# Seven block products for the down-projection of two FFN parts, with x streamed through DRAM

## The chip, the cores and the metric

One core of a Trainium2 chip runs one program. The metric is the device time of one execution in microseconds, and the verdict compares the kernel after with the kernel before on the same chip. Three runs of the kernel before are shown, and one profiled execution.

## What is computed

One step of a decoder trunk over 520 tokens (512 new ones of a sequence and 8 single ones) and a model width of 1024: half an FFN, a mixer of attention and state-space heads, half an FFN, a final norm. The change lies in the two FFNs, which are

```
h = rmsnorm(x, norm_g)
gate, up = split(h @ w_in)
x = x + 0.5 * ((silu(gate) * up) @ w_out)
```

with `w_in` of 1024 x 5632 and `w_out` of 2816 x 1024. All is float32 in and out.

## The kernel before

Everything is kept transposed: x is eight tiles of 128 features x 520 tokens, and the 2816 hidden features are 22 tiles `j`. A float32 product is made of three matmuls on TensorE: a value is split into a high part and a rest (`cut`, line 355, for weights: a cast on ACT, line 357, and a subtraction on DVE, line 358), and high x high, high x low and low x high are added in PSUM (`mm3`, lines 225 to 227; `product`, lines 579 to 581). Each matmul takes 128 x 128 weights and 260 tokens, half of the 520 (`HF`).

`ffn_comb` does one FFN. The hidden tiles come in four parts, `PARTS = ((0, 6), (6, 12), (12, 18), (18, 22))`. In each part the gate and up values of its tiles are computed, and then the part's share of the down-projection is added to x (the "down" stage, PSUM tiles `fo`, line 471 reads them). Tiles 0 to 4 use plain products. From tile 5 on (`SFROM`), gate and up are computed together as a 2 x 2 block product with seven multiplications in place of eight (Strassen's scheme in Winograd's form): `combos` prepares combinations of the normalised input once, `b_split` combinations of the weights for each `j`, and `comb_pair` (line 584) does the products 1, 5, 2, 6, 3, 7 in the PSUM banks `cx`, `cy`, `cz`; product 4 follows within the next pair or the down stage, in `comb_last` (line 608). Sums are kept in PSUM: bank x takes products 1, 6, 7 and 4 one after another, and between them ACT or DVE read it. After product 1, ACT copies x to bank z (line 590), after product 6 it copies x (line 596), and DVE reads x after product 7 (line 603) and after product 4 (line 612). The finished hidden tile is split again (`hidh`, line 615, and `hidl`, line 616).

The down stage of a part of six tiles takes 8 rows `m` of x, two halves, six tiles and three matmuls. Its weights come as eight "dn" units, 768 columns each, loaded as 512 and 256. Rows of x stay in SBUF: `reload` (line 1445) fetches all eight at the end of the first part, from the input or, in the second FFN, from the DRAM tile `spill`.

The order of TensorE's instructions is the order of the program text (`manual_schedule`); a scheduler orders the other engines and the DMA queues by program order and readiness, each queue in order. `stream` (line 303) lists the weight units with a cost; `b_more` (line 401) cuts further units while those cut and not yet taken are worth less than `AHEAD = 10` us; `b_load` (line 330) loads two units further. A pair's unit is five loads on SP's queue and two accumulating loads on POOL's (lines 350 to 352); DVE adds two more combinations (lines 384 and 386). The buffers are rings: 12 raw weight tiles (`r`), 14 + 12 cut ones (`q`, in the pools `pf` and `pg`), 58 general tiles of 528 columns (`t2`), and eight PSUM banks.

Of the kernel before, what the change touches and what calls it, by code (L numbers as in the profile page):

```python
# [14 lines left out]
T = 520  # L15
NP = 512
HF = 260
# [6 lines left out]
SRAW = 3  # L24
AHEAD = 10.0
# [60 lines left out]

def layout(inp):
# [5 lines left out]
    for n, s in (("ffn1", "1"), ("ffn2", "2")):  # L93
        out["wi" + s] = c(g[f"w_{n}_in"][0].reshape(8, 128, 2, 22, 128).transpose(3, 2, 1, 0, 4)).reshape(44, 128, 1024)
        out["wo" + s] = c(g[f"w_{n}_out"][0].reshape(22, 128, 8, 128).transpose(2, 1, 0, 3)).reshape(8, 128, 2816)
# [52 lines left out]
class Program:  # L148
# [147 lines left out]
    def stream(self, s):  # L296
        a = self.a
        wi, wo = a["wi" + s], a["wo" + s]
        u = []
        for lo, hi in PARTS:  # L300
            for j in range(lo, hi):
                if j < SFROM:
                    u += [("cl", wi[2 * j + i], 1024, 5.8) for i in range(2)]
                else:
                    u.append(("pair", wi[2 * j], wi[2 * j + 1], 10.1))
            if s == "1" and hi == PARTS[-1][1]:
                break
            u += [("dn", wo[m][:, lo * 128:hi * 128], (hi - lo) * 128, 0.72 * (hi - lo)) for m in range(8)]
        self.bu = u
        self.b_raw, self.b_w = {}, {}  # L310
        self.b_limit = 2 if s == "2" else len(u)
        self.b_first = 8 * (s == "2")
        self.b_q = self.b_loaded = self.b_cut = self.b_taken = 0

    def q2(self, name):
        n = self.b_q - self.b_first
        self.b_q += 1
        if self.qpool is not None:
            pool = self.qpool
        elif n < 0:  # L320
            pool = self.p0
        else:
            pool = self.pf if n < 12 or n % 7 % 2 == 0 else self.pg
        return pool.tile([128, 512], F32R, name=name, tag="q")

    def r2t(self, name):
        first = self.b_loaded <= 2 and self.b_first
        return (self.p0 if first else self.pf).tile([128, 512], F32, name=name, tag="r", bufs=4 if first else 12)

    def b_load(self):  # L330
# [15 lines left out]
        g, u = p  # L346
        h = slice(0, 512), slice(512, 1024)
        g0, s1, s3, g1, u1 = t = [self.r2t(f"br{n}_{i}") for i in range(5)]
# [12 lines left out]
    def b_split(self):  # L361
# [11 lines left out]
        else:  # L373
            g0, s1, s3, g1, u1 = raw
            s2, s4 = self.t2("s2"), self.t2("s4")
            w = {}
            ends = self.b_cut == len(self.bu), self.b_cut == len(self.bu) - 1
            if self.b_first == 0 and any(ends):
                self.qpool = self.pf
            w[1], w[5] = self.cut(g0), self.cut(s1)  # L380
            if self.b_first == 0 and ends[0]:
                self.qpool = self.pg
            w[2] = self.cut(g1)
            nc.vector.tensor_add(s2[:, :512], s1, g0)
            w[6] = self.cut(s2)
            nc.vector.tensor_add(s4[:, :512], s2[:, :512], g1)
            w[3], w[7] = self.cut(s4), self.cut(s3)
            if self.b_first == 0 and ends[1]:
                self.qpool = self.pg
            w[4] = self.cut(u1)  # L390
# [15 lines left out]
    def ffn_comb(self, gcol, source, after=None, early=None):  # L406
# [3 lines left out]
        with self.tc.manual_schedule(engines={mybir.EngineType.PE}):  # L410
            hid, held, r, norm = [], None, None, None
            for j in range(SFROM):
                pair = []
                if j == 0:
# [6 lines left out]
                    if self.b_first:  # L421
                        self.leave("p0")
                        self.enter("pg", 12, "right")
# [23 lines left out]
            prev = None  # L447
            for part, (lo, hi) in enumerate(PARTS):
                for j in range(max(lo, SFROM), hi):
                    prev = self.comb_pair(j, prev, hid)  # L450
                last = part == len(PARTS) - 1
                if part == 0:
                    self.reload(source)
                tail, prev = prev, None
                if last and after is None:
# [4 lines left out]
                for m in range(8):  # L460
                    w = self.w_take() if last else self.b_take()
                    ps = [self.bank1("fo") for _ in range(2)]
                    nk = hi - lo
# [5 lines left out]
                    for f in range(2):  # L469
                        x = self.x[m][:, f * HF:(f + 1) * HF]  # L470
# [8 lines left out]
                hid = []  # L479

    def to_mixer(self):

        self.leave("pf")
# [4 lines left out]
        for _ in range(2):  # L488
            self.w_split()

# [54 lines left out]
    def combos(self):  # L545
# [4 lines left out]
        for i in range(4):  # L550
            c = self.cx[i]
            c[1] = [t[:, a] for t in self.h[i]]
# [19 lines left out]
    def product(self, out, w, p, start):  # L572
# [3 lines left out]
        for i in range(4):  # L576
            xh, xl = self.cx[i][p]
# [3 lines left out]
            mm(out, lhsT=lo[:, ks], rhs=xh, start=False, stop=i == 3, skip_group_check=True)  # L581

    def comb_pair(self, j, prev, hid):
# [5 lines left out]
        self.product(x, w, 1, True)  # L589
        nc.scalar.copy(z, x)  # L590
        self.product(y, w, 5, True)
        nc.scalar.copy(pu[:, a], y)
        self.product(z, w, 2, False)
        nc.scalar.activation(c[:, a], z, AF.Silu)
        self.product(x, w, 6, False)
        nc.scalar.copy(pu[:, b], x)
        if prev is not None:
            self.comb_last(prev, hid)
        self.product(y, w, 3, False)
        nc.vector.tensor_add(c[:, b], y, pu[:, b])  # L600
        nc.scalar.activation(c[:, b], c[:, b], AF.Silu)
        self.product(x, w, 7, False)
# [3 lines left out]
        return x, w, c  # L606

    def comb_last(self, prev, hid):
        nc = self.nc
        x, w, c = prev  # L610
        self.product(x, w, 4, False)
        nc.vector.scalar_tensor_tensor(c[:, :HF], x, -1.0, c[:, :HF], ALU.mult, ALU.mult)
        hh = self.t2("hidh", F32R)
# [3 lines left out]
        hid.append((hh, hl))  # L617

# [901 lines left out]
    def run(self):  # L1520
        nc, tc, a = self.nc, self.tc, self.a
        with (
# [8 lines left out]
            self.enter("pf", 14)  # L1531
            self.enter("pg", 12, "right")
# [39 lines left out]
            def early():  # L1572
                self.leave("pg")
# [19 lines left out]
            self.enter("pf", 14)  # L1593
# [5 lines left out]
            self.leave("pg")  # L1599
            self.leave("pf")  # L1600
# [18 lines left out]
```

## Time and profile before

| what | us |
|---|---|
| median of the runs shown | 1125.81 |
| lowest and highest of the three | 1122.23, 1126.17 |
| the profiled execution | 1118.79 |
| its span in the profile | 1117.0 |
| TensorE busy | 1080.7 |
| VectorE busy | 719.4 |
| ScalarE busy | 501.6 |

The first FFN fills the span from about 8 us to 374 us, the mixer follows, and the second FFN runs from about 740 us to the end. In the rows, PE is TensorE's matmuls and PEld its weight loads, DVE is VectorE, ACT ScalarE, POOL GpSimd, and SPq a queue of DMA issues. A row of a timeline gives the start, the length and the instruction, in brackets the idle time before it and what ended it. Matmuls are pipelined and overlap in the records, and their ends are modelled.

### The profile page before, as it was taken

The page shows a single profiled execution, that of the slowest core. Times are in us where ns is not written, and L with a number is a line of the kernel's source. Part 1 is how long each engine was busy: PE and PEld are TensorE (multiplying, and loading weights), DVE is VectorE, ACT ScalarE, POOL GpSimd, SP SyncE. Part 2 cuts the span into 40 slices and gives each one's busy share as a digit, 9 for nine tenths or more (in the row PEclk, how much of TensorE's full clock was granted, in tenths as well). Part 3 has the DMA queues.
Part 4 walks back from the last instruction along what each step waited for, and adds up shares of the span by engine and source line. Part 5 has one row for each costly group of instructions (what it writes and reads, how often), then busy time and mean ns, then how long its engine had stood idle before and what let it go on. Part 6 is the DMA issues. An engine that isn't in the chain of part 4 may idle for free. (4 is left out here: it accounts for less than half of the span.)

```text
span 1117.0 us, 23260 instructions
## 1 busy us (share of the span) xinstructions
PE 1080.7 (97%) x9079; PEld 997.0 (89%) x9079; DVE 719.4 (64%) x1499; ACT 501.6 (45%) x1077; POOL 261.3 (23%) x261
## 2 busy tenths in 40 slices
PE   7999999999999999999989998999999999999995
PEld 6999999999999978676756776999999999999995
DVE  6985576467556678264677758449855774685563
ACT  6452454356245422356623554245533543562452
POOL 0001001010106668476234321030010011101013
PEclk8999999999999999899999997999999999999997
DMA  7538458456617889589899643264393584666302
GB/s 270 136 116 240 101 133 231 107 134 174 153 39 237 269 283 316 186 277 322 318 386 381 236 170 122 70 206 121 107 250 90 143 224 102 147 172 154 106 10 77
DMA packets 93917, 204.30 MB, mean 183 GB/s; under 512 B 13384, under 2 KB 21960, under 8 KB 89712
## 3 DMA queue, kind: packets, MB, share of 16 engines
q1 hardware_dynamic: 68736, 124.19, 34.1%
q0 software_dynamic: 22336, 77.08, 24.8%
q10 hardware_dynamic: 2736, 1.56, 0.5%
q8 instruction: 71, 1.16, 0.4%
q14 instruction: 38, 0.31, 0.1%
HBM read 191.78 MB, written 11.01 MB: 182 GB/s over the span
## 5 line engine op out<-in xcount | busy, mean ns | idle before, releaser
L357 ACT CAST qh<-br 128x512 fp32r<-128x512 f32 (+1 forms) x310 | 168.1, 585 | 121.0 <-PE fo L226 65.5
L358 DVE TENSOR_TENSOR ql<-br,qh 128x512 fp32r<-128x512 f32 (+1 forms) x310 | 189.2, 648 | 45.9 <-ACT qh L357 20.2
L226 PE MATMUL fo<-hidl,qh 128*128 128x260 f32 x640 | 181.3, 283 | 0.8 <-DVE hidl L616 0.8
L225 PE MATMUL fo<-hidh,qh 128*128 128x260 f32 x640 | 181.2, 283 | 0.0
L227 PE MATMUL fo<-hidh,ql 128*128 128x260 f32 x640 | 180.9, 283 | 0.0
L579 PE MATMUL cx<-ch,qh 128*128 128x260 f32 x544 | 153.7, 283 | 0.0
L581 PE MATMUL cx<-ch,ql 128*128 128x260 f32 x544 | 153.6, 282 | 0.0
L580 PE MATMUL cx<-cl,qh 128*128 128x260 f32 x544 | 153.6, 282 | 0.0
L226 PEld LDWEIGHTS fo<-hidl,qh 128*128 128x128 f32 x640 | 120.5, 188 | 1.5 <-DVE hidl L616 1.4
L225 PEld LDWEIGHTS fo<-hidh,qh 128*128 128x128 f32 x640 | 120.5, 188 | 0.0
L227 PEld LDWEIGHTS fo<-hidh,ql 128*128 128x128 f32 x640 | 120.5, 188 | 0.0
L225 PE MATMUL mps<-hh,whi 128*128 128x260 f32 x384 | 112.2, 292 | 1.6 <-DVE fdq L875 1.3
L351 POOL DMA_DIRECT2D br<-in_wi x34 | 29.7, 873 | 352.9 <-DMA br<-in_wi 232.2
L226 PE MATMUL mps<-hl,whi 128*128 128x260 f32 x384 | 108.6, 283 | 0.6 <-DVE hl L236 0.6
L227 PE MATMUL mps<-hh,wlo 128*128 128x260 f32 x384 | 108.4, 282 | 0.0
L579 PEld LDWEIGHTS cx<-ch,qh 128*128 128x128 f32 x544 | 102.4, 188 | 0.0
L581 PEld LDWEIGHTS cx<-ch,ql 128*128 128x128 f32 x544 | 102.4, 188 | 0.0
L580 PEld LDWEIGHTS cx<-cl,qh 128*128 128x128 f32 x544 | 102.3, 188 | 0.0
L789 POOL DMA_INDIRECT kv<-in_kc,ix x66 | 72.1, 1092 | 66.9 <-PE cy L581 25.7
L225 PEld LDWEIGHTS mps<-hh,whi 128*128 128x128 f32 x384 | 72.2, 188 | 13.4 <-issue 10.2
L579 PE MATMUL cy<-ch,qh 128*128 128x260 f32 x272 | 77.0, 283 | 0.0
L580 PE MATMUL cy<-cl,qh 128*128 128x260 f32 x272 | 77.0, 283 | 0.0
(430 smaller groups left out, 2721.9 us busy)
## 6 DMA issues: line engine op xcount, KB each, us to landing
br<-in_wi SPq DMA_DIRECT2D x206, 256.0 KB, 3.8
br<-in_wi POOLq DMA_DIRECT2D x68, 256.0 KB, 5.4
br<-in_wo SPq DMA_DIRECT2D x56, 256.0 KB, 2.9
wraw<-in_wm SPq DMA_DIRECT2D x24, 512.0 KB, 5.9
br<-in_wo SPq DMA_DIRECT2D x48, 128.0 KB, 2.7
kv<-in_kc SPq DMA_DIRECT2D x22, 256.0 KB, 4.3
spill<-xr SPq DMA_DIRECT2D x16, 260.0 KB, 2.0
xr<-spill SPq DMA_DIRECT2D x16, 260.0 KB, 5.1
```

The lines of the kernel that those rows point to most:

```text
L225: mm(out, lhsT=hi[:, ks], rhs=xh[:, cs], start=start, stop=False)
L226: mm(out, lhsT=hi[:, ks], rhs=xl[:, cs], start=False, stop=False)
L227: mm(out, lhsT=lo[:, ks], rhs=xh[:, cs], start=False, stop=stop)
L351: nc.gpsimd.dma_start(s1, u[:, h[1]], accum_op=ALU.add)
L357: self.nc.scalar.copy(hi[:, :n], raw[:, :n])
L358: self.nc.vector.tensor_sub(lo[:, :n], raw[:, :n], hi[:, :n])
L579: mm(out, lhsT=hi[:, ks], rhs=xh, start=start and i == 0, stop=False, skip_group_check=True)
L580: mm(out, lhsT=hi[:, ks], rhs=xl, start=False, stop=False, skip_group_check=True)
L581: mm(out, lhsT=lo[:, ks], rhs=xh, start=False, stop=i == 3, skip_group_check=True)
L789: nc.gpsimd.indirect_dma_start(out=pages[j], out_offset=None, in_=a["kc"], in_offset=bass.IndirectOffsetOnAxis(ap=self.ix[:, 4 * n + j:4 * ...
```

## The change

The down stage of parts 2 and 3 (six tiles each, `COMB = (1, 2)`) becomes a 2 x 2 block product with seven multiplications, in both FFNs. A row pair `m`, `m + 1` is one unit of weights with halves of 384 columns, and the rows of `w_out` are put in another order on the host so that tiles `j` and `j + 1` fall into the two halves. `hidden` combines each two finished hidden tiles into the seven input blocks; three blocks make a part. `down_comb` does the products of a row pair in the order 1, 5, 2, 6, 3, 7, 4 in the banks `dx`, `dy`, `dz`, and runs after the first pair of the next part.

x no longer stays in SBUF. In parts 1 to 3 each row is loaded (`x_load`, four buffers), added to and stored in `spill`; `reload` stands in the last part and reads `spill`. In `comb_pair`, product 4 of the pair before moves ahead of product 2 (it stood after product 6). In `b_split` the cuts are put in the order 1, 5, 2, 6, 3, 7, 4. `combos` copies half of the first four input tiles into tiles of their own (`p1`). The rings become 10 raw and 11 + 9 cut tiles, with a pool `py` of two for the sums of weights.

```diff
@@ stream
+            if part in COMB:
+                return [("pair", w[m], w[m + 1], n // 2, 1.26 * (hi - lo)) for m in range(0, 8, 2)]
...
+                if j == lo and part - 1 in COMB:
+                    u += down(part - 1)
@@ ffn_comb
+                if part:
+                    hid = []
                 for j in range(max(lo, SFROM), hi):
-                    prev = self.comb_pair(j, prev, hid)
...
+                    prev = self.comb_pair(j, prev, hx if prev and j == lo else hid, comb)
+                    if j == lo and todo is not None:
+                        self.down_comb(hx, prev, hid)
+                        hx, todo, prev = [], None, None
+                if comb:
+                    hx, todo = hid, part
+                    continue
...
+                if last:
+                    self.reload(self.spill)
...
+                    xm = self.x[m] if last else self.x_load(m, source)
...
+                        nc.sync.dma_start(self.spill[m], xm[:, :T])
@@ new functions
+    def x_load(self, m, source):
+        x = self.px.tile([128, 528], F32, name=f"xs{m}", tag="x")
+        self.nc.sync.dma_start(x[:, :T], source[m])
+        return x
+
+    def down_comb(self, hx, tail, hid):
...
+        for m in range(0, 8, 2):
+            w = self.b_take()
+            x, y, z = (self.bank1(n)[:, :HF] for n in ("dx", "dy", "dz"))
+            x0, x1 = self.x_load(m, self.spill), self.x_load(m + 1, self.spill)
+            pu = self.t2("pu")
+            self.product(x, w, 1, True, hx)
+            nc.scalar.copy(z, x)
+            self.product(y, w, 5, True, hx)
+            nc.scalar.activation(pu[:, a], y, AF.Copy, scale=-0.5)
+            if m == 0:
+                self.comb_last(tail, hid)
+            self.product(z, w, 2, False, hx)
+            stt(x0[:, a], z, 0.5, x0[:, a], ALU.mult, ALU.add)
+            self.product(x, w, 6, False, hx)
+            nc.scalar.activation(pu[:, b], x, AF.Copy, scale=0.5)
+            self.product(y, w, 3, False, hx)
+            stt(x0[:, b], y, 0.5, x0[:, b], ALU.mult, ALU.add)
+            nc.vector.tensor_add(x0[:, b], x0[:, b], pu[:, b])
+            nc.sync.dma_start(self.spill[m], x0[:, :T])
+            self.product(x, w, 7, False, hx)
+            stt(x1[:, b], x, -0.5, x1[:, b], ALU.mult, ALU.add)
+            nc.vector.tensor_add(x1[:, b], x1[:, b], pu[:, a])
+            self.product(x, w, 4, False, hx)
+            stt(x1[:, a], x, -0.5, x1[:, a], ALU.mult, ALU.add)
+            nc.sync.dma_start(self.spill[m + 1], x1[:, :T])
+            self.b_more()
+
+    def hidden(self, c, hx):
...
+        if not hx or len(hx[-1]) > 1:
+            hx.append({0: c})
+            return
+        x0, x1 = hx.pop()[0], c
+        p1 = self.t2("p1", F32R)
+        nc.scalar.copy(p1[:, a], x0[:, a])
+        nc.vector.tensor_sub(p1[:, b], x0[:, a], p1[:, a])
+        s, t = self.t2("hs"), self.t2("ht")
+        nc.vector.tensor_sub(s[:, a], x0[:, a], x0[:, b])
+        nc.vector.tensor_sub(s[:, b], x1[:, b], x0[:, b])
+        nc.vector.scalar_tensor_tensor(t[:, a], s[:, b], -1.0, x0[:, a], ALU.mult, ALU.subtract)
+        nc.vector.scalar_tensor_tensor(t[:, b], t[:, a], -1.0, x1[:, a], ALU.mult, ALU.subtract)
+        q = self.two(s, x1, t)
...
@@ comb_pair
+        if prev is not None:
+            self.comb_last(prev, hid)
...
-        if prev is not None:
-            self.comb_last(prev, hid)
@@ combos
-            c[1] = [t[:, a] for t in self.h[i]]
+            p1 = self.t2("p1", F32R)
+            for z, t in zip((a, b), self.h[i]):
+                nc.scalar.copy(p1[:, z], t[:, a])
+            c[1] = p1[:, a], p1[:, b]
@@ rings
+        self.enter("pf", 11)
+        self.enter("px", 4)
+        self.enter("pg", 9, "right")
+        self.enter("py", 2, "right")
```

`two` casts whole tiles of 520 columns on ACT and subtracts on DVE (line 537); `product` takes its input blocks as an argument, four for a pair and three here.

## Rows read from the trace of the kernel before

**Rows 1.** The page's first line and its busy times: us, share of the span, instructions.
```profile
span 1117.0 us, 23260 instructions
...
PE 1080.7 (97%) x9079; PEld 997.0 (89%) x9079; DVE 719.4 (64%) x1499; ACT 501.6 (45%) x1077; POOL 261.3 (23%) x261
```

**Rows 2.** Stretches in one pair stage and one down stage, with their column line.
```profile
core 0: us, PE busy (x) PEld busy (x) DVE busy (x) ACT busy (x) POOL busy (x), PEclk, DMA share, GB/s
123.00:173.00 50.00, 50.00 (x419) 50.00 (x418) 36.89 (x69) 30.87 (x68) 4.18 (x5) 1.00 0.51 129
182.00:213.00 31.00, 30.82 (x256) 30.82 (x257) 14.33 (x31) 7.24 (x13) 4.31 (x5) 1.00 0.63 138
```

**Rows 3.** Waits, PE for the hidden tile: us in total, times, longest us.
```profile
PE fo L226 <- DVE hidl L616: 1.2, 3, 0.5
```

**Rows 4.** Timeline: last matmul of a product 4, and DVE's read of it.
```profile
239.11 0.28 PE L581 MATMUL cx<-ch,ql 128*128 128x260 f32 x1
...
239.44 0.43 DVE L612 SCALAR_TENSOR_TENSOR cg<-cx,cg 128x260 f32<-128x260 f32 x1 [1.83 <-PE cx L581]
```

**Rows 5.** Groups by line and shape: count, busy us, mean ns, idle time before.
```profile
L358 DVE TENSOR_TENSOR ql<-br,qh 128x512 fp32r<-128x512 f32 x262 | 172.2, 689 | 41.6 <-ACT qh L357 19.1 <-issue 9.6 <-PE fo L227 7.5
...
L357 ACT CAST qh<-br 128x512 fp32r<-128x512 f32 x262 | 152.9, 618 | 97.9 <-PE fo L226 57.1 <-DMA br<-in_wi 15.8 <-issue 12.4
...
L471 DVE SCALAR_TENSOR_TENSOR xr<-fo,xr 128x260 f32<-128x260 f32 x112 | 43.4, 426 | 31.7 <-PE fo L227 31.6
...
L358 DVE TENSOR_TENSOR ql<-br,qh 128x256 fp32r<-128x256 f32 x48 | 20.2, 420 | 4.2 <-PE cx L580 2.6 <-ACT qh L357 1.1 <-issue 0.3
...
L590 ACT COPY cz<-cx 128x260 f32<-128x260 f32 x34 | 12.4, 364 | 53.3 <-PE cx L581 53.2
```

**Rows 6.** Timeline: PE waits for DVE's hidden tile and starts again.
```profile
181.41 0.28 PE L225 MATMUL fo<-hidh,qh 128*128 128x260 f32 x1
...
181.44 0.69 DVE L616 TENSOR_TENSOR hidl<-cg,hidh 128x520 fp32r<-128x520 f32 x1
...
182.19 0.39 PE L226 MATMUL fo<-hidl,qh 128*128 128x260 f32 x1 [0.49 <-DVE hidl L616]
...
182.41 0.28 PE L227 MATMUL fo<-hidh,ql 128*128 128x260 f32 x1
```

**Rows 7.** Waits, DVE's read after product 7 in the pair stage.
```profile
DVE pu L603 <- PE cx L581: 2.4, 7, 0.6
```

**Rows 8.** Timeline of PE and ACT around one late copy from x to z.
```profile
233.24 0.28 PE L581 MATMUL cx<-ch,ql 128*128 128x260 f32 x1
...
234.38 0.37 ACT L590 COPY cz<-cx 128x260 f32<-128x260 f32 x1
...
234.81 0.38 PE L579 MATMUL cz<-ch,qh 128*128 128x260 f32 x1
235.03 0.28 PE L580 MATMUL cz<-cl,qh 128*128 128x260 f32 x1
```

**Rows 9.** The page's DMA queues, and issues: KB each, us to landing.
```profile
q1 hardware_dynamic: 68736, 124.19, 34.1%
q0 software_dynamic: 22336, 77.08, 24.8%
...
xr<-spill SPq DMA_DIRECT2D x16, 260.0 KB, 5.1
```

**Rows 10.** Waits, DVE's addition of a tile that POOL accumulates.
```profile
DVE s L384 <- DMA br<-in_wi: 25.9, 6, 7.5
```

**Rows 11.** Stretches in the mixer, columns as in rows 2; timeline at the lower clock.
```profile
610.00:615.00 5.00, 4.53 (x39) 1.91 (x37) 4.23 (x13) 2.66 (x7) 4.03 (x4) 1.00 0.79 270
...
684.00:688.00 4.00, 2.82 (x6) 1.23 (x7) 4.00 (x10) 1.85 (x3) 0.00 (x0) 0.50 0.00 0
...
11.12 0.42 PE L225 MATMUL gu<-hh,qh 128*128 128x260 f32 x1
11.34 0.42 PE L226 MATMUL gu<-hl,qh 128*128 128x260 f32 x1
```

More of the change, by code (lines that the diff above doesn't have):

```diff
@@ L24 @@
 SRAW = 3
+COMB = (1, 2)
 AHEAD = 10.0
@@ L84, in shape_constants, with hidden_order @@
     return f, b.astype(mybir.dt.np(BF16)), i3, r
+def hidden_order():
+    o = []
+    for part, (lo, hi) in enumerate(PARTS):
+        o += [j for i in range(2) for j in range(lo + i, hi, 2)] if part in COMB else range(lo, hi)
+    return o
 def layout(inp):
@@ L299, in stream, with down @@
         u = []
-        for lo, hi in PARTS:
+        def down(part):
+            lo, hi = PARTS[part]
+            n = 128 * (hi - lo)
+            w = [wo[m][:, lo * 128:hi * 128] for m in range(8)]
+            if part in COMB:
+                return [("pair", w[m], w[m + 1], n // 2, 1.26 * (hi - lo)) for m in range(0, 8, 2)]
+            return [("dn", w[m], n, 0.72 * (hi - lo)) for m in range(8)]
+        for part, (lo, hi) in enumerate(PARTS):
             for j in range(lo, hi):
@@ L304, in stream @@
                 else:
[L305 to L308, printed above, removed]
+                    u.append(("pair", wi[2 * j], wi[2 * j + 1], 512, 10.1))
+                if j == lo and part - 1 in COMB:
+                    u += down(part - 1)
+            if part not in COMB and not (s == "1" and hi == PARTS[-1][1]):
+                u += down(part)
         self.bu = u
@@ L327, in r2t @@
         first = self.b_loaded <= 2 and self.b_first
[L328 removed]
+        return (self.p0 if first else self.pf).tile([128, 512], F32, name=name, tag="r", bufs=4 if first else 10)
     def b_load(self):
@@ L570, in combos, with product @@
         halves(self.two(*tt), 6, 4)
-    def product(self, out, w, p, start):
+    def product(self, out, w, p, start, blocks):
         mm = self.nc.tensor.matmul
         hi, lo = w[p]
-        for i in range(4):
-            xh, xl = self.cx[i][p]
+        last = len(blocks) - 1
+        for i, block in enumerate(blocks):
+            xh, xl = block[p]
             ks = slice(128 * i, 128 * i + 128)
@@ L605, in comb_pair @@
         self.b_more()
-        return x, w, c
+        return x, w, c, comb
     def comb_last(self, prev, hid):
         nc = self.nc
-        x, w, c = prev
-        self.product(x, w, 4, False)
+        x, w, c, comb = prev
+        self.product(x, w, 4, False, self.cx)
         nc.vector.scalar_tensor_tensor(c[:, :HF], x, -1.0, c[:, :HF], ALU.mult, ALU.mult)
+        if comb:
+            self.hidden(c, hid)
+            return
         hh = self.t2("hidh", F32R)
```

90 lines of the change are left out of this document (51 added, 39 removed).

## The prediction

> **What bounds the kernel now.** I read the page's busy times first. TensorE (PE) is busy for 1080.7 of a span of 1117.0 us, VectorE (DVE) for 719.4 and ScalarE (ACT) for 501.6 [rows 1]. PE's matmul ends are modelled, so 97% alone proves little; the second view is a table of stretches. In the stretch of input-projection pairs (123 to 173 us) PE issues 419 matmuls in 50 us, one every 0.119 us. In a down-projection stretch (182 to 213 us) it issues 256 in 31 us, the same pace, while DVE works 14.3 of 31 us [rows 2]. The list of waits says the same: in both FFNs' down-projections PE waited for the hidden tile in three places, 1.2 us in all [rows 3]. So time in these stages is the number of matmuls times 0.119 us, plus whatever makes PE stand still. The change lowers the first and, as I read the code, raises the second.
>
> **Matmuls removed.** A part of six hidden tiles took 8 output rows x 6 tiles x 2 halves x 3 matmuls = 288. Now it is 4 row pairs x 7 products x 3 blocks x 3 = 252. That is 36 fewer per part, and four parts change: 144 x 0.119 = 17.2 us less.
>
> **The wait that is added.** In `down_comb` product 7 accumulates in bank x, DVE reads x, and product 4, the very next instruction on PE, goes on accumulating in x. PE's order is written by hand, so nothing comes between them. In the pair stage product 4 is put off into the next pair, so no row shows this exact wait; its pieces are there. DVE starts 0.33 us after the start of the last matmul that it waits for (239.11 to 239.44) [rows 4]. Such a read of 260 columns takes 0.426 us [rows 5]. A PE that waited for DVE restarts 0.06 us after DVE's end (181.44 + 0.69 = 182.13, then 182.19), and its second matmul comes 0.22 us later, not 0.12 [rows 6]. Together 0.33 + 0.43 + 0.06 = 0.82, less the 0.12 that the next matmul would have had anyway, is 0.70; with the slow restart 0.80 us. Four row pairs in four parts make 16 of them: 12.8 us with DVE free. What the slow restart is worth can be argued: the Trainium skill (TensorE: Matmul & The Clock Gate, "Step-by-step: what each phase is for") says that the next weights are loaded while the present matmul runs, so that they would be in place after the wait. By that the wait is 0.70 us and the sum 11.2; the row has the 0.22, and I go by the row.
>
> **DVE is not always free.** Per row pair it now has seven subtractions and two additions of 384 columns, and six operations of 260. The rows give 0.420 us at 256 columns and 0.689 at 512 [rows 5], so about 0.55 at 384: 9 x 0.55 + 6 x 0.43 = 7.5 us in a period of 63 x 0.119 + 0.8 = 8.3 us. Records of neighbours overlap a little, so some 80% busy against 46% in the old stage [rows 2]. In the pair stage, at 74%, the matching read after product 7 found DVE idle 7 times in 34 (one per pair, the count in [rows 5]) [rows 7]; otherwise it ran behind something. An operation in the way costs between 0 and 0.55 us; I take 0.8 x half of 0.55, about 0.22. x 16 = 3.5 us (bounds 0 and 8.8).
>
> **ACT's copies.** Product 1 must be copied from x to z before product 2, with only product 5 between. That was 12 matmuls in a pair and is 9 here: 10 x 0.119 - 0.33 - 0.36 - 0.06 = 0.44 us to spare. The trace has a pair in which ACT came 0.81 us late (233.24 + 0.33, then 234.38): with 12 matmuls PE lost just the 0.10 of a slow restart (234.81 to 235.03) [rows 8]; with 9 it would lose 0.46. Product 6 has the same spare time before product 7. I take one such loss in four row pairs: 4 x 0.46 = 1.8 us (bounds 0 and 2 x 16 x 0.46 = 14.7). In the 34 pairs the copy to z gains time, since product 4 of the pair before now stands ahead of product 2, and the copy of x after product 6 loses it: 13 x 0.119 - 0.33 - 0.36 - 0.06 = 0.80 us left. One pair in five at 0.10 us is 0.7 us.
>
> **Part ends.** The last hidden tile of a combined part is now ready a whole pair before its use: after product 4 there are four products of 12 matmuls (5.7 us) and six more matmuls. Its chain is one read, four 260-column DVE steps, and for the last operands a cast of about 0.62 and a subtraction of 0.69, some 3.5 us alone. p1 is wanted first and is made first. I cost it at nothing, and the waits of [rows 3] go for the combined parts: -0.8 us. If DVE were 3 us behind there, it would cost up to 2 us in each of four places.
>
> **Transfers.** x is no longer loaded once per FFN: parts 1 to 3 load and store all eight rows, and part 4 reloads them. That is 24 loads and 24 stores more per FFN, 48 x 260 KB twice. A combined part loads 20 tiles of 384 columns and eight accumulating ones in place of 16. Per row pair that is 5 x 192 KB + 4 x 260 KB on SP's queue, 2.05 MB, and 0.39 MB on POOL's. SP's queue moved 124.19 MB in 34.1% of the span, 326 GB/s; POOL's 77.08 in 24.8%, 278 GB/s [rows 9]: 6.3 + 1.4 = 7.7 us of engine time in 8.3 us. So the queues just hold, and rows move up and down. A row's x is asked for up to two row pairs ahead (four buffers) and lands in about 5 us [rows 9], DVE is its only reader, so it is covered by some 8 us of products. The stores wait for DVE on SP's queue, and the weight loads issued behind them wait too; what reads those is the cuts, one unit ahead of PE. I take 1 us (bounds 0 and the third rival). The reload, moved to the last part, is covered by eight PSUM banks; the eight p1 copies in `combos` (8 x 0.36 us on ACT [rows 5]) fall under two plain tiles of 11 us each, and the smaller rings (20 weight tiles for 26) still hold a unit of 14 and three products. All at nothing.
>
> **Sum.** -17.2 - 0.8 + 12.8 + 3.5 + 1.8 + 0.7 + 1.0 = +1.8 us. The profiled execution took 1118.8 us, 1.8 more than its span, so it would become 1120.6. It was 7 us below the median of the runs shown, 1125.8; the same difference there gives 1127.6, and I say 1128.
>
> **The rivals.** *First, the waits are smaller* (1117 us). The ends of matmuls are modelled, so the 0.33 us and the slow restart may be partly drawing; at half of 0.80 us with DVE on time, the balance is -17.2 - 0.8 + 6.4 + 2.5 = -9. For it: DVE's idle time before the read of product 4 shows it answering at once in the pair stage [rows 4]. Against it: a 260-column read alone is 0.43 us and can't shrink.
>
> *Second, the weights come late* (1140 us), the slower side. Where a pair's tile is loaded and then accumulated by POOL, DVE stood six times, up to 7.5 us, at the addition that reads it [rows 10], always where units changed from down to pair. The old stage hid this behind PSUM banks. Now every row pair has such tiles, at 8 us distance instead of 10, and whatever stops DVE stops product 4 at once. It decides from a lateness of more than the half microsecond that is left: 3 us in each of the four parts is +12. Against it: in the steady pair stage DVE shows no such wait.
>
> *Third, the combined hidden tiles come late* at the four part ends: +8, 1134 us. Against it: 6 us of cover for a chain of 3.5.
>
> *Fourth, the clock.* From 684 to 688 us, where PE did 6 matmuls in 4 us, the granted clock was 0.50, the lower level of 1.2 GHz; from 610 to 615, with 39 in 5 us and PE idle now and then, it was 1.00 [rows 11]. At the lower level a matmul takes 0.22 us (11.12 to 11.34) [rows 11], so a stage of 63 matmuls would lose 6 us; half of 16 row pairs is +49, 1177 us. The Trainium skill (TensorE: Matmul & The Clock Gate, "A second HAM failure mode: psum-queue depth-cycling") warns of just this, small idle times between groups of matmuls that let the clock swing. With some 30 matmuls in 4 us the new stage lies near the stretch that kept 1.00.
>
> *Fifth, the change doesn't do what it says*: PE's pace is set elsewhere and the fewer matmuls bring nothing. The even 0.119 us in both stages speaks against it; no change, 1126.
>
> **How the numbers follow.** Forecast 0.45 (its own range 1122 to 1134, from the bounds of DVE and ACT), smaller waits 0.20, late weights 0.22, late hidden tiles 0.07, clock 0.02, no effect 0.04. About 0.5% (5.6 us) is what a measurement of this kernel can tell from no change. Faster by more: the first rival, 0.20. Within: forecast less its upper tail, no effect and part of the third, 0.45. Slower: late weights, clock, the rest, 0.35. The range of 1117 to 1140 takes in most of both sides.
>
> **What would show it.** Right: matmuls down by 144 in all; in the list of waits sixteen waits of PE on tile dx for DVE, 0.4 us or more each in the profile's idle time, some 7 us or more together; down stages of combined parts near 34 us, as before. Wrong: dx waits absent or below 3 us (first rival), DVE idle for DMA ahead of its additions inside `down_comb` (second), PE waiting for ch or cl at the start of dx products (third), a granted clock below 1.00 there (fourth).

## The result, and the profile after

The changed kernel took 1149.82 us (median of 4 runs, 1142.57 to 1154.08) against 1124.02 before: a ratio of 1.0243 [1.0209, 1.0278]. The forecast of 1128 and its range, up to 1140, were both too low. The profiled execution took 1153.84, and its span is 35.1 us longer than before. The medians differ by less, 25.8 us: the profiled execution of the kernel before, 1118.79, lies below its four runs, and that of the changed kernel among the longest of its own. The rows and the balance below are those of the two profiled executions.

The page of the changed kernel: span, busy times, and the first DMA queue.

```profile
span 1152.1 us, 23785 instructions
...
PE 1081.3 (94%) x8935; PEld 991.0 (86%) x8935; DVE 799.4 (69%) x1683; ACT 559.7 (49%) x1213; POOL 287.7 (25%) x293
...
q1 hardware_dynamic: 84864, 152.90, 40.8%
```

The 144 matmuls are gone [rows 1], and yet PE's busy time is no shorter: busy time stretches where the clock is low (below). DVE does 80 us more. The list of waits (total, times, longest), PE's first:

```profile
PE dx L659 <- DVE xs L543: 17.5, 16, 3.4
PE cx L659 <- DVE pu L683: 13.7, 3, 9.5
...
PE cz L659 <- ACT cz L670: 3.4, 1, 3.4
```

The first row is the wait that the prediction counted, sixteen times (the "dx waits" below). The other two were not there before, and they are in the gate-and-up pairs, which the change hardly touches. The largest of them in the timeline (start, duration, in brackets the idle time before and what ended it):

```profile
882.50 0.28 PE L661 MATMUL cy<-ch,ql 128*128 128x260 f32 x1
892.32 0.58 PE L659 MATMUL cx<-ch,qh 128*128 128x260 f32 x1 [9.53 <-DVE pu L683]
```

DVE, which PE waited for, had itself been waiting, for a tile of weights:

```profile
875.02 1.29 DVE L378 TENSOR_TENSOR ql<-s,qh 128x512 fp32r<-128x512 f32 x2 [0.44 <-ACT qh L377]
888.49 0.69 DVE L405 TENSOR_TENSOR s<-br,br 128x512 f32<-128x512 f32 x1 [12.18 <-DMA br<-in_wi]
889.10 0.68 DVE L378 TENSOR_TENSOR ql<-br,qh 128x512 fp32r<-128x512 f32 x1
```

The stop that ends at 143 us has the same shape: DVE stood for 7.0 us at L405. No releaser is named there, but SP issued nothing from 128.7 to 133.7 us, and then a load of x. At 331 us ACT stood 6.7 us for such a tile (it casts the tiles first). Why the tile is late can be read from SP, which issues all these loads. Its timeline before the large stop:

```profile
868.63 0.32 SPq L515 DMA_DIRECT2D xs<-spill  x1
869.04 0.38 SPq L370 DMA_DIRECT2D br<-in_wi  x1
869.52 0.38 SPq L505 DMA_DIRECT2D spill<-xs  x1
870.02 0.35 SPq L370 DMA_DIRECT2D br<-in_wi  x1
874.48 0.32 SPq L515 DMA_DIRECT2D xs<-spill  x1
874.90 0.37 SPq L505 DMA_DIRECT2D spill<-xs  x1
875.71 0.85 SPq L370 DMA_DIRECT2D br<-in_wi  x2
878.26 0.33 SPq L515 DMA_DIRECT2D xs<-spill  x1
878.68 15.67 SPq L370 DMA_DIRECT2D br<-in_wi  x10
```

Loads of x (L515) stand between the loads of weights (L370), and from 870.4 to 874.5 nothing is issued at all. SP's own waits name the reason, and the row is absent before:

```profile
SPq L515 <- DMA spill<-xs: 121.6, 39, 5.4
```

and the page gives the time that a store takes to land (the last figure, median us):

```profile
spill<-xs SPq DMA_DIRECT2D x48, 260.0 KB, 5.3
```

A load of x waits until a store of x has landed, either the store that frees its buffer or the store of the same row; whatever stands behind it on SP waits too. After such a stop the clock is low. Stretches around 887 us (columns as in [rows 2], the last three being granted clock, DMA share and GB/s):

```profile
881.00:887.00 6.00, 1.78 (x15) 1.57 (x13) 0.00 (x0) 0.00 (x0) 1.52 (x2) 1.00 0.89 250
887.00:892.00 5.00, 0.00 (x0) 0.00 (x0) 3.51 (x7) 1.26 (x3) 0.86 (x1) 0.50 0.83 162
892.00:897.00 5.00, 4.68 (x21) 4.69 (x22) 4.59 (x12) 3.01 (x8) 0.86 (x1) 0.50 0.81 206
897.00:902.00 5.00, 5.00 (x43) 5.00 (x42) 4.08 (x8) 3.93 (x9) 0.86 (x1) 0.97 0.70 157
```

The granted clock fell while PE stood and was still at its lower level, 1.2 GHz, for 5 us after it went on: 21 matmuls where the next stretch has 43. The same follows the stops that end at 143.3, 330.9 and 980.7 us. In the four places PE worked 3.0 + 3.1 + 4.8 + 5.3 us at one matmul in 0.22 us in place of 0.12, which cost about 7 us.

Two more costs have no row in the list of waits. A matmul's record lasts 0.28 us though the next one can start after 0.12, so a stop costs 0.16 us more than the idle time shown for it. And ACT's copies hold PE up a little without any idle time. Both show in one row pair:

```profile
225.31 0.38 ACT L537 ACTIVATE pu<-dx 128x260 f32<-128x260 f32 x1
...
225.54 0.28 PE L661 MATMUL dy<-ch,ql 128*128 128x260 f32 x1
225.75 0.39 PE L659 MATMUL dx<-ch,qh 128*128 128x260 f32 x1
225.97 0.28 PE L660 MATMUL dx<-cl,qh 128*128 128x260 f32 x1
...
226.81 0.28 PE L661 MATMUL dx<-ch,ql 128*128 128x260 f32 x1
...
227.60 0.39 PE L659 MATMUL dx<-ch,qh 128*128 128x260 f32 x1 [0.52 <-DVE xs L543]
227.83 0.28 PE L660 MATMUL dx<-cl,qh 128*128 128x260 f32 x1
```

The copy ends at 225.69; product 7 starts 0.09 us late and its second matmul 0.10 us late. Such pieces ahead of products 2 and 7 add up to 2.3 us in the sixteen row pairs. Product 4 starts 0.79 us after the matmul before it, where 0.12 is the pace: 0.67 us lost, with an idle time of 0.52, and then the slow restart, 0.23 us to the second matmul.

That makes the balance. Removed matmuls -17.2; dx waits +17.5, with 16 x 0.16 for the overlap of records and 16 x 0.10 for the restarts, 21.7; waits in the pairs 13.7 + 3.4 and 4 x 0.16, 17.7; ACT's copies +2.3; low clock +7: together some +32. By landmarks (the first matmul on tile mps, the last on tile gu, the end) FFN1 became 12.7 us longer, the mixer with FFN2's plain tiles 3.5, and the rest of FFN2 18.9. So of the 35.1 us, 3.5 lie where nothing was changed, and the terms with a row to their name make up the rest to within 1 us. That it comes out so close is partly luck: ends of matmuls are modelled, and the clock's term is rounded.

### The profile page after: what moved, and what is told of

It reads as the page before. It is cut to its first block, busy times and chain, and to the rows that moved or that the text cites. A ratio compares the mean times of both kernels' runs of the same rounds, so it can differ in the third digit from the quotient of the medians.

```text
span 1152.1 us, 23785 instructions
## 1 busy us (share of the span) xinstructions
PE 1081.3 (94%) x8935; PEld 991.0 (86%) x8935; DVE 799.4 (69%) x1683; ACT 559.7 (49%) x1213; POOL 287.7 (25%) x293
## 5 line engine op out<-in xcount | busy, mean ns | idle before, releaser
L377 ACT CAST qh<-br 128x512 fp32r<-128x512 f32 (+2 forms) x326 | 186.2, 583 | 163.6 <-PE fo L237 30.4
L378 DVE TENSOR_TENSOR ql<-br,qh 128x512 fp32r<-128x512 f32 (+2 forms) x326 | 206.0, 642 | 74.6 <-ACT qh L377 32.5
L659 PE MATMUL cx<-ch,qh 128*128 128x260 f32 x408 | 116.8, 286 | 13.7 <-DVE pu L683 13.7
L660 PE MATMUL cx<-cl,qh 128*128 128x260 f32 x408 | 116.4, 285 | 0.0
L661 PE MATMUL cx<-ch,ql 128*128 128x260 f32 x408 | 116.2, 285 | 0.0
L377 ACT CAST qh<-s 128x512 fp32r<-128x512 f32 (+1 forms) x100 | 57.1, 585 | 43.2 <-PE dx L661 18.2
L378 DVE TENSOR_TENSOR ql<-s,qh 128x512 fp32r<-128x512 f32 (+1 forms) x100 | 63.7, 644 | 20.2 <-ACT qh L377 6.4
L661 PE MATMUL cy<-ch,ql 128*128 128x260 f32 x272 | 77.0, 283 | 0.0
L236 PEld LDWEIGHTS mps<-hl,whi 128*128 128x128 f32 x384 | 72.3, 188 | 1.2 <-DVE hl L246 1.1
L236 PE MATMUL fo<-hidl,qh 128*128 128x260 f32 x256 | 72.6, 284 | 0.6 <-DVE hidl L699 0.6
L235 PE MATMUL fo<-hidh,qh 128*128 128x260 f32 x256 | 72.6, 283 | 0.0
```

Of the source, the lines that this page charges most:

```text
L235: mm(out, lhsT=hi[:, ks], rhs=xh[:, cs], start=start, stop=False)
L236: mm(out, lhsT=hi[:, ks], rhs=xl[:, cs], start=False, stop=False)
L377: self.nc.scalar.copy(hi[:, :n], raw[:, :n])
L378: self.nc.vector.tensor_sub(lo[:, :n], raw[:, :n], hi[:, :n])
L659: mm(out, lhsT=hi[:, ks], rhs=xh, start=start and i == 0, stop=False, skip_group_check=True)
L660: mm(out, lhsT=hi[:, ks], rhs=xl, start=False, stop=False, skip_group_check=True)
```

## The experiments

Two theories stood at first. A: the sixteen fixed waits after product 7 are the cost. B: late data is the cost, and with it the stops. Each run has its own measurement of the kernel before on the same chip; ratios are to that, and kernels measured at different times are compared by their ratios. In the diffs, "..." stands for lines left out.

**1. Product 4 covered.** In `down_comb`, product 6 moves ahead of 2 and 7 ahead of 3, so that product 3 stands between DVE's read of product 7 and product 4 (only the products are shown; what reads each moves with it):

```diff
+            self.product(x, w, 6, False, hx)
...
             self.product(z, w, 2, False, hx)
...
-            self.product(x, w, 6, False, hx)
...
+            self.product(x, w, 7, False, hx)
...
             self.product(y, w, 3, False, hx)
...
-            self.product(x, w, 7, False, hx)
...
             self.product(x, w, 4, False, hx)
```

> In the row pairs of the combined down-projection the products are put in the order 1, 5, 6, 2, 7, 3, 4, so that product 3 lies between product 7 and product 4 while VectorE reads bank x. Theory A (product 4 right behind product 7 costs most of the added time): the sixteen waits of the changed kernel, 17.5 us of idle time and about 0.26 us of restart each, some 22 us, nearly vanish; the median goes from 1150 to 1126 to 1132 us. Theory B (late weights and what they do to the clock cost most): the dx waits shrink but the time stays above 1140 us, since the three waits of the pair stage (13.7 us) and the clock's falls remain. If VectorE is simply behind everywhere, the waits move to other products and less than 8 us is won.

Measured: 1143.56, ratio 1.0219 [1.0169, 1.0268], not clearly below the changed kernel's 1.0243. The waits of this kernel:

```profile
PE dx L659 <- DVE xs L539: 15.7, 6, 5.4
PE cx L659 <- DVE pu L683: 10.4, 3, 7.1
```

The fixed waits are gone, sixteen have become six, but the six are just as long together. So the order of products costs something only where DVE is on time; here it wasn't.

**2. x of part 1 kept in SBUF.** Part 1 no longer streams x; it loads all eight rows at once, as the kernel before did, and stores them as they are finished:

```diff
+                elif part == 0:
+                    self.reload(source)
...
-                    xm = self.x[m] if last else self.x_load(m, source)
+                    xm = self.x[m]
```

> Only the first part of each FFN goes back to the x of the kernel before: all eight rows are loaded at the end of its pairs into general tiles and stored to DRAM after use, without the ring of four buffers. Theory B (x loads that wait for one of four buffers at the head of SP's queue hold up the weight loads behind them): PE's waits on VectorE's read after product 7 in the pair stage (13.7 us in three places) and the clock's falls after them go, 15 to 25 us of the profiled 1153.8; median 1128 to 1138. Rival (the smaller rings of raw and cut weights hold up the loads): no change within 4 us. Theory A predicts that the sixteen dx waits stay at 15 to 20 us.

Measured: 1131.11, ratio 1.0103 [1.0075, 1.0131]: of the changed kernel's 2.4%, 1.4% are gone. In the waits of this kernel the long ones in the pairs are gone but for one, and those of dx are as they were:

```profile
PE dx L661 <- DVE xs L545: 15.6, 16, 2.7
PE cz L661 <- ACT cz L672: 3.9, 1, 3.9
PE cx L661 <- DVE pu L685: 0.3, 1, 0.3
```

Streaming x in part 1, which has no block product, is thus over half of the loss.

**3. Product 4 late again.** In the pair stage the change puts product 4 of the pair before ahead of product 2; this puts it back behind product 6.

```diff
-        if prev is not None:
-            self.comb_last(prev, hid)
         self.product(z, w, 2, False, self.cx)
...
         nc.scalar.copy(pu[:, b], x)
+        if prev is not None:
+            self.comb_last(prev, hid)
```

> Only the place of product 4 of the pair before goes back to behind product 6. If moving it 24 matmuls (2.9 us) forward is what exposed PE to a late VectorE, the waits of 3.8 and 9.5 us become about 1 and 6.6 us, and the clock falls one time less: 5 to 10 us faster than 1150. If the lateness of the weights alone decides, the wait moves and the gain is below 3 us.

Measured: 1149.65, ratio 1.0266 [1.0235, 1.0297], the same as the changed kernel. Where PE stood moved from the read of product 7 to the copy of z (14.8 us in 4). A late tile is late wherever PE meets it.

**4. Streaming alone.** No block product in the down-projection at all, the old 9079 matmuls, but x streamed in parts 1 to 3 and the smaller rings:

```diff
-COMB = (1, 2)
+COMB = ()
...
-                    xm = self.x[m] if last else self.x_load(m, source)
+                    xm = self.x[m] if last else self.x_load(m, self.spill if part else source)
```

> The changed kernel with its set of combined parts empty: all parts are plain down-projections (288 matmuls each again), while x is streamed with four buffers, the rings are the smaller ones and product 4 stands where the change put it. Theory A alone: no dx waits, so the time of the kernel before, 1124 us, within 5 us. Theory B: the pair stage behind the parts that stream x waits for late weights as before the experiment, 8 to 20 us above 1124, with falls of the clock.

Measured: 1155.54, ratio 1.0306 [1.0253, 1.0359]: as slow as the whole change or slower, and more than the 8 to 20 us that theory B had forecast. Waits of PE in this kernel:

```profile
PE cx L659 <- ACT pu L678: 15.8, 2, 10.4
PE cx L659 <- DVE pu L683: 9.8, 2, 5.0
```

and the wait of SP behind them:

```profile
SPq L515 <- DMA spill<-xs: 149.8, 40, 6.1
```

**5. The smaller rings alone**, in the kernel before: ten raw tiles for twelve, 20 cut tiles for 26:

```diff
-        return (self.p0 if first else self.pf).tile([128, 512], F32, name=name, tag="r", bufs=4 if first else 12)
+        return (self.p0 if first else self.pf).tile([128, 512], F32, name=name, tag="r", bufs=4 if first else 10)
...
-            self.enter("pf", 14)
-            self.enter("pg", 12, "right")
+            self.enter("pf", 11)
+            self.enter("pg", 9, "right")
```

> The kernel before with the smaller rings of the change alone (10 raw tiles for 12, 11 + 9 cut tiles for 14 + 12), nothing else. If the rings are what makes weights late, it loses 10 us or more against 1121; the theory of SP's queue says they don't matter: within 4 us of the kernel before.

Measured: 1121.72, ratio 0.9995 [0.9965, 1.0024]. Without streamed x they cost nothing.

**6. Streaming alone with eight buffers** for x in place of four:

```diff
-            tc.tile_pool(name="p2", bufs=58) as self.p2,
+            tc.tile_pool(name="p2", bufs=54) as self.p2,
...
-        self.enter("px", 4)
+        self.enter("px", 8)
```

> The kernel of e4 (x streamed, no combined parts, 1155.5 us) with eight x buffers in place of four, paid for by four general tiles fewer (54 for 58). Theory B1: x loads wait on SP's queue for one of four buffers, that is for a store to land, and weight loads stand behind them; with eight buffers no load of a part has to wait for a store of the same part, and the time falls by 20 us or more, to 1120 to 1135. Theory B2: the transfers themselves are too many for the DMA engines: the time stays above 1145.

Measured: 1153.18, ratio 1.0284 [1.0249, 1.0318], a miss for the idea that four buffers are too few. The time lies where theory B2, too many bytes, had it; experiment 9 decides on that. SP's wait is still there:

```profile
SPq L515 <- DMA spill<-xs: 118.5, 31, 6.3
```

With eight buffers, the loads for the next part take their place in SP's order right behind the stores, and wait for their own row to land. More buffers can't cure that: the wait stands in the queue, not in the ring.

**7. Covered product 4 with eight buffers** for x: the edit of 1 and the last diff together.

> The changed kernel with the product order of e1 and eight x buffers (54 general tiles). B1 and A together: 1143.6 less some 20 us of late weights and of the clock's falls, and no dx wait of more than 1 us: 1108 to 1125. If B2 holds: above 1135.

Measured: 1137.48, ratio 1.0141 [1.0102, 1.018]; a miss, and again in B2's range: 84.4 us in 31 waits of that kind are left.

**8. Experiments 1 and 2 together:** both diffs in one kernel.

> e1 and e2 together: product 3 between 7 and 4, and the first part's x in general tiles. If the sixteen waits (15.5 us of idle time in e2, and 0.26 us of restart each, some 19 us) are paid in full on top of e2's 1131, the time is 1112 to 1118, and the kernel before (1121) is beaten. If lateness moves the waits to other products as it did in e1, 1122 to 1128.

Measured: 1128.25, ratio 1.0058 [1.002, 1.0095], just above the second range. The waits in the pairs are down to 2.1 us, but dx waits of 16.2 us in 8 are left. From 200 to 230 us, in the row pairs, the DMA share is 1.01 at 290 GB/s.

**9. The same bytes, no wait for a landing.** This tells waiting in the queue from bandwidth. It is experiment 6 with other addresses (`away` is a second DRAM tile like `spill`):

```diff
-                    self.reload(self.spill)
+                    self.reload(source)
...
-                    xm = self.x[m] if last else self.x_load(m, self.spill if part else source)
+                    xm = self.x[m] if last else self.x_load(m, source)
...
-                        nc.sync.dma_start(self.spill[m], xm[:, :T])
+                        nc.sync.dma_start(self.away[m], hid[0][0].bitcast(F32)[:, :T])
```

> No block products; x streamed in parts 1 to 3 with eight tiles, as in the run that took 1153 with that ring, and the same bytes moved; but no transfer waits for a store to land: the loads come from the FFN's input always, and the stores write a tile of hidden values to a place that nobody reads. So the output leaves out the first three parts' sums. Theory of the queue's head: SP's queue no longer stands at loads that wait for a store's landing (118.5 us in 31 waits with the stores read back), weights come in time: 1120 to 1132, no stop of TensorE over 3 us in the gate-and-up products of part 2. Rival, the bytes: 64 rows of 266 KB in and out of memory beside the weights use up the transfers' rate, wherever they wait: 1143 to 1156.

Measured: 1123.73, ratio 1.0031 [1.0011, 1.005]; 229.90 MB were moved, as in experiment 6. The row `DMA spill<-xs` is gone from SP's waits. SP still stands for DVE's additions to x, 96.7 us in 52 waits, but 1.9 us at a time where the waits for landings in experiment 6 took 3.8:

```profile
SPq L370 <- DVE xs L503: 58.4, 25, 4.9
SPq L515 <- DVE xs L503: 38.3, 27, 4.4
```

The stretches of this kernel in which the changed one had its first stop (columns as in [rows 2]):

```profile
80.00:115.00 35.00, 35.00 (x293) 35.00 (x292) 20.34 (x41) 9.93 (x18) 4.98 (x6) 1.00 0.75 198
115.00:145.00 30.00, 30.00 (x253) 30.00 (x252) 21.46 (x38) 17.68 (x37) 4.49 (x6) 1.00 0.87 240
```

PE is never idle in them. So the bytes of the stream, with the smaller rings and the other order of products, cost 0.3%, and the waiting on SP's queue the other 2.5%, some 28 us. (The stores here also wait for no addition. In experiment 6 SP stood 26.2 us at stores for additions beside the 118.5 us for landings; what each of the two costs isn't parted by a run. Nor was the direct test made, x's loads on a queue on which no weights stand.)

**10. x stays.** With that known, x should not travel at all: eight tiles per FFN hold it through parts 1 to 3, and only part 3's rows are stored, for the reload. Product 4 is covered as in experiment 1, and the rings are those of experiment 6.

```diff
+                elif part == 0:
+                    self.xp = [self.x_load(m, source) for m in range(8)]
...
-                        nc.sync.dma_start(self.spill[m], xm[:, :T])
...
-            x0, x1 = self.x_load(m, self.spill), self.x_load(m + 1, self.spill)
+            x0, x1 = self.xp[m:m + 2]
...
-            nc.sync.dma_start(self.spill[m], x0[:, :T])
...
+            if store:
+                nc.sync.dma_start(self.spill[m], x0[:, :T])
```

> Block products in parts 2 and 3 with product 4 behind product 3 (the order 1, 5, 6, 2, 7, 3, 4); x is loaded once per FFN into eight tiles, the sums of parts 1, 2 and 3 stay in them, and only the third part's rows are stored for the last part to reload. Ring of tiles p2 is 54. Theory: in the row pairs the transfers are at their limit (DMA share 1.01 and 290 GB/s from 200 to 230 us with the same order and x streamed, 16.2 us of waits on the additions to x in that profile, three falls of the clock of 3.4 us) because x's four transfers of 266 KB per row pair come on top of the tiles of weights; without them the additions come in time. Then the waits of the dx bank on xs sum to under 6 us, the low-clock stretches of the FFNs go, and the time is 1104 to 1116. Rival: VectorE's own work in the row pairs (22 of 30 us busy) makes the additions late whatever the transfers do: waits of 10 us or more stay, 1120 to 1128. Mean granted clock 0.98 by the theory.

Measured: 1119.96, ratio 1.0 [0.9979, 1.0021]. All of the loss is undone, but nothing is won, a miss by 4 us; the rival on VectorE's own work had the waits, 10 us or more. What PE waited for:

```profile
PE dx L662 <- DVE xs L540: 10.3, 6, 3.2
```

and DVE, for tiles of weights:

```profile
DVE s L405 <- DMA br<-in_wi: 20.2, 8, 3.7
```

The dx waits are 1.0 us in FFN1 and 9.3 in FFN2. By the same landmarks FFN1 is 5.8 us shorter than before in this profile (367.5 for 373.3), the mixer 3.2 longer, with no edit there, and the rest of FFN2 2.8 longer. DVE has the same operations in both FFNs' row pairs, so its own work alone doesn't explain the 9.3. In FFN2 the timeline shows the addition s at 1029.77 after 3.67 us of waiting for a tile whose accumulating transfer POOL had issued at 1023.28, and the read of product 7 behind it: PE then waited 2.88 us, up to 1033.32. The other two long ones, up to 937.97 and 1044.39, stand behind such tiles too (3.62 us at 934.42, 3.17 at 1040.56).

**11. x stays, old order of products:** experiment 10 without the diff of experiment 1.

> As the run before it, but with the changed kernel's own order of the products (7 behind 3, 4 behind 7). Theory: the order's 16 waits of product 4 on the addition read by product 7's bank are fixed work between the engines, 16 x (0.75 + 0.26 us) = 16 us in the changed kernel and no matter of transfers, so this is 8 to 16 us slower than the run before it and its dx waits number 16 with each at least 0.4 us. Rival: those waits were long only because VectorE stood for late weights; without x's transfers they shrink to under 6 us in all and the two runs lie within 4 us.

Measured: 1127.69, ratio 1.0078 [1.0042, 1.0115], and `dx` waits of 15.0 us in 16. This is the price of product 4 behind product 7 with x out of the way: 7.7 us in medians, just under the 8 to 16 that were expected.

**12. GpSimd adds in the row pairs.** The sums of weight blocks, which an accumulating transfer makes, are made by GpSimd from four loaded tiles:

```diff
+        if w < 512:
+            for d, src in ((g0, g[:, h[0]]), (s1, u[:, h[0]]), (u1, u[:, h[1]]), (g1, g[:, h[1]])):
+                nc.sync.dma_start(d, src)
+            nc.gpsimd.tensor_add(s3, s1, g0)
+            nc.gpsimd.tensor_add(s1, s1, u1)
```

> As the run with x kept in eight tiles and product 4 behind product 3, and in the row pairs' weights the two sums of blocks are made by GpSimd additions from four loaded tiles, in place of five loaded tiles and two transfers that accumulate. Per row pair that is four transfers of 192 KB for seven: 16 x 3 x 0.197 = 9.4 MB less, 222.3 to 212.9 MB. GpSimd: an issue of an accumulating transfer took 0.86 us, an addition of 128x512 1.29 us and of 128x260 0.74 us, so some 1.0 us each, 32 of them, about as before. Theory: what is left of the dx waits (10.3 us in 6, 9 of them in FFN2, where the VectorE addition s2 waits up to 3.7 us for a late tile) is the weights' tiles coming late; with three transfers in seven gone the waits fall under 4 us and the time is 1107 to 1115. Rival: VectorE's own work sets the additions (26 of 30 us busy from 200 to 230 us): waits of 8 us or more stay, 1117 to 1122.

Measured: ratio 1.0034 [1.0006, 1.0062]. Measured beside it, the kernel before, too, took 1153.48 us (on the same chip, beside experiments 1 to 4, 1120.97), so only the ratio is of use; in the trace the mixer, where nothing was changed, is 21 us longer than in experiment 10, and the waits compare only roughly. The dx waits stay at 10.4 us in 9, as the rival had it, though 9.4 MB less were moved. But the tiles that DVE's addition waited for (19.9 us in 8) are all those of gate-and-up units, which still accumulate.

**13. GpSimd adds everywhere**, and **14. the same in the kernel before:** the diff of 12 without its first line, so that no unit accumulates any more.

> x kept in eight tiles, product 4 behind product 3, and the two sums of blocks made by GpSimd in every unit, gate-and-up units too, so that no transfer accumulates. Theory: the dx waits that stay (10.3 us) come from the accumulating transfer, which starts only when its tile has landed and lands some 6 us later (issued at 1023.28, used at 1029.77); a GpSimd addition takes 1.3 us in its place. Then the waits of VectorE's addition s on tiles of weights fall under 1 us each, the dx waits under 4 us, and the ratio to the kernel before is 0.984 to 0.994. Rival: VectorE's own work in the row pairs (26 of 30 us) makes the additions late: dx waits of 8 us or more, ratio 0.998 to 1.004. Second rival: GpSimd's additions slow VectorE's, its subtraction of 128x512 rises above 0.68 us by over 0.05, and the ratio is above 1.0.

> The kernel before with the two sums of blocks made by GpSimd in place of accumulating transfers, and nothing else changed. Its TensorE has no stop over 0.5 us in the row products and none over 1 us in the gate-and-up products of parts 2 and 3, so an earlier tile has nothing to give back: ratio 0.997 to 1.003 by the theory. If it is 0.994 or below, what the run beside it gains is not owed to the block products.

Measured: 13 has a ratio of 1.0035 [1.0015, 1.0055], 14 of 1.0054 [1.0034, 1.0073]. The late tiles are cured: `DVE s` waiting for `br` is absent from 13's list. But the groups by line and shape (count, busy us, mean ns) show what took its place. DVE in 13:

```profile
L378 DVE TENSOR_TENSOR ql<-br,qh 128x512 fp32r<-128x512 f32 x230 | 175.9, 778 | 34.5 <-ACT qh L377 17.0 <-PE cx L663 5.8 <-PE fo L236 3.6
L378 DVE TENSOR_TENSOR ql<-br,qh 128x384 fp32r<-128x384 f32 x80 | 53.5, 679 | 1.0 <-PE cy L664 0.4 <-ACT qh L377 0.2
```

and GpSimd's additions there:

```profile
L371 POOL TENSOR_TENSOR br<-br,br 128x512 f32<-128x512 f32 x34 | 49.8, 1466 | 327.9 <-DVE ql L378 293.5 <-DMA br<-in_wi 28.2 <-DVE xs L541 6.1
```

The subtraction of 128x512 took 0.689 us before [rows 5] and in experiment 10 and now takes 0.778; that of 128x384, 0.551 in experiment 10, takes 0.679. DVE is busy 860.0 us for 799.5, and PE's dx waits are 11.6 us in 11: in FFN2, where the late tiles were, they fell from 9.3 to 5.7 us, in FFN1 they rose from 1.0 to 5.9. The second rival of that expectation held. The first one's numbers (8 us or more, 0.998 to 1.004) came out as well, but DVE's instructions are those of experiment 10, where FFN1 lost only 1.0 us, so their number alone doesn't explain the waits. In 14, expected to change nothing, the subtraction of sums took 0.893 for 0.686, and the kernel before got slower: a miss, by the same cause. No version tried beats the kernel before.

## Why the prediction was wrong

**Matmuls removed: right.** 8935 for 9079, and the pace at full clock is the same: 294 matmuls from 80 to 115 us in both kernels.

**The added wait: right in kind, too small in size.** The forecast for the wait and DVE's lateness, 12.8 + 3.5 = 16.3 us, counts from one matmul's start to the next and has the slow restart in it. Counted so, the sixteen waits cost 21.7 us, of which 17.5 show as idle time. The slow restart came (227.60, then 227.83 us). A part of this is late weights, as the 3.4 us wait at 980.66 shows: DVE had stood 2.57 us for a tile at 975.56. What the order alone costs is experiment 11 against 10: 7.7 us.

**ACT's copies: right in the row pairs; part ends: right.** The copies cost 2.3 us there against 1.8, but in many pieces of some 0.1 us and not in four losses of 0.46. No wait for ch or cl appeared at the part ends; of the 0.8 us to be won there 0.3 came (PE's waits for hidl: 1.2 us before, 0.9 after).

**Transfers: the step that failed.** It said that a row's x "is covered by some 8 us of products", that what reads the weights behind the stores is "the cuts, one unit ahead of PE", and "I take 1 us". It checked that the queues hold the bytes, and they do (experiment 9: 0.3%). What it left out is what the loads themselves wait for. A load of x on SP waits for a store to land, about 5 us after a store that itself waits for an addition; SP stands 121.6 us in 39 such waits with the weights behind it, the lead of one unit is used up, and stops of 3.4 to 9.5 us follow. Its upper bound there, the third rival (+8 us), priced late hidden tiles and not late weights. The prediction looked at the row pairs; more than half of the damage came from part 1 (experiment 2), whose eight streamed rows it took to be free. The price of streaming without block products was +34.6 us (experiment 4), of which 0.3% or some 4 us remain when SP doesn't wait (experiment 9); the prediction had +1.

**The second rival** had the mechanism, late weights, and DVE's addition as its sign [rows 10], but the wrong cause and place: accumulating tiles in the row pairs, at 3 us in each part. That fits what is left once x stays (experiment 10), some 10 us; the one cure tried (experiment 13) slowed DVE as well, so no run shows the price of those tiles by itself. **The first rival**'s smaller waits didn't come. **The fourth**, given 0.02 at 49 us, priced a swinging clock in the row pairs; what came was a low clock during and after each long stop, some 7 us, while in the row pairs from 200 to 230, 296 to 324 and 1052 to 1080 us the granted clock stayed 1.00. The low clock is a consequence of lateness, and should have been part of the second rival's price.

The sum corrected, for the two profiled executions: -17.2 for matmuls, +21.7 for the order and DVE (16.3 forecast), +2.3 for ACT's copies, +25 for the stops and the clock that the streamed x causes (17.7 + 7; 1 forecast), and 3.5 in the mixer: +35 for the 35.1 measured.

Still open is whether FFN2's late tiles in experiment 10 could be cured without burdening DVE, with more raw tiles for instance; that wasn't tried.

## What to carry to other kernels

Before sending a resident tile through memory, look at what each new transfer waits for and what stands behind it on its queue, not only at the bytes: a load that waits for a store's landing stops every load after it. Price a stop of TensorE with its low clock. And when an algebraic saving needs tiles that the kernel has no room for, price the room first: here 17.2 us of matmuls did go, and with x kept in place and product 4 covered the kernel was still no faster than before.

## What the runs showed of the hardware

- A stop of TensorE of 9.5 us cost 2.2 us more through the clock: the granted clock was 0.50 from 887 to 897 us, and PE worked from 892.3 to 897.1 at one matmul in 0.22 us for 0.12.
- GpSimd's additions and VectorE's two-input operations slow each other (experiments 13 and 14): the subtraction took 0.778 us for 0.689 (128x512) and 0.679 for 0.551 (128x384), and an addition of 128x512 on GpSimd 1.47 us on average, where additions of that size in the mixer of the kernel before took 1.29. The subtraction of sums of 128x512 kept its 0.684 us in 13 and rose to 0.893 in 14. The Trainium skill (SBUF — State Buffer, "Who interferes with whom") says that a VectorE instruction with both inputs in SBUF contends with GpSimd's reads. The rows agree.
- Bytes alone were cheap: 25.6 MB more (experiment 9, 229.90 for 204.30 MB) cost 0.3%, and 36 MB less (experiment 13 against 10, 186.11 for 222.30 MB) gained nothing, with DVE slower beside it.
